# Last up product, first activations and first weights of down: one written order, and other tiles to load into

## The chip, the cores and the metric

The kernel runs on one core of a Trainium2 chip. What is compared is the time of one execution on the device, in microseconds (us). The core has TensorE (PE, with its weight loads shown apart as PEld), VectorE (DVE), ScalarE (ACT), GpSimd (POOL) and SyncE (SP), which issues most of the transfers. Each engine takes its own instructions in order and waits on semaphores for the others.

## The reference

One inference step of a one-layer decoder trunk: modulation from the conditioning vector, a norm, an input projection, a short convolution beside dilated window attention, an output projection with a gated residual, and then the part that this case is about:

```
h2 = rmsnorm(x, norm2_g) * (1 + sc2) + sh2          # x is [1056 tokens, 1024]
ffn = (silu(h2 @ w_gate) * (h2 @ w_up)) @ w_down    # w_gate, w_up [1024, 2816]; w_down [2816, 1024]
x = x + ga2 * ffn
y = rmsnorm(x, final_g)
```

1024 tokens are the prompt and 32 are the samples. Everything is float32.

## The kernel before

Each float32 matrix product is made of three matmuls on operands that are split in two: a high part (names ending in `h` or `hi`), which ACT makes by a copy into a rounded type, and a low part (`l` or `lo`), which DVE makes by subtracting the high part from the original. A weight tile is loaded into a `raw` tile, ACT writes `wh` from it and DVE writes `wl`; an activation tile `a` gives `ah` and `al` in the same way. So a tile is ready for PE only after a transfer, one ACT and one DVE instruction.

**Gate and up.** The hidden width is walked in eleven steps `f` (0 to 10, `FH` = 11). For each `f`, `ffn_pair` makes the gate product and then the up product of two lanes (the two halves of the tokens), each with `block_product`. One `block_product` has seven steps; in each step a half `wh`, `wl` of a weight tile multiplies a block of each lane in 12 matmuls of 264 columns, and the sums go to PSUM banks 0, 1, 0, 2, 0, 2, 0 of the lane (named `pss`, `pspt`, `psmm`). The weights come through `weight_units`: the raw tiles `r1` (pool `wp`, three places) and `r2` (pool `w3`, three places) are loaded by SP, POOL makes sums and differences of their quarters, and ACT and DVE split them. After a step `hold` copies a bank by ACT (`p1`, `u2`, `p5` in the code, `p` and `u` in the profile), or `put` adds by DVE and multiplies into the tile `sg`. At the end of `f` POOL stores `sg` in DRAM (`a_d`).

**Down.** The eleven `f` form chunks of 3, 3, 3 and 2. For a chunk, `load_a` brings its activations back from `a_d` (for the first chunk six tiles of 128x1056) through places of the `raw` tag of `wp` and splits them into `ah` and `al`, which take the places of the operands of up (`ua`, `ub`). Then, for each of the eight column blocks `m`, `load_down` brings 128x768 weights through the same `raw` places, and `down` makes three blocks of tokens (384, 384 and 288) of 18 matmuls each; `add_gated` adds each block to a tile of the residual (`x2` in the code, `x` in the profile), which SP loads from `xT_d` in the first chunk. The PSUM tiles of down take turns between the tags of `psmm` (two places) and `pss` (three places).

**Order.** A scheduler orders the instructions of each engine at build time by its own estimates; `tc.high_priority()` moves work ahead, `in_order(x)` makes an instruction stand behind another, and `program_order()` makes the instructions of PE, DVE, ACT and POOL that are recorded inside it stand in the order in which the code records them (SP is not among them). The code of `load_a` and `load_down` stood after the whole of gate and up.

Of the kernel before, what the change touches and what calls it, by code (L numbers as in the profile page):

```python
# [59 lines left out]
def hybrid_step(  # L60
# [1257 lines left out]
    def weight_units(w, f):  # L1318

        with tc.high_priority():  # L1320
            r1 = load_raw(w[:, :, P * f:P * f + P], KT)
            r2 = w3.tile([P, KT, P], F32, tag="raw", bufs=3, name=nm("raw"))
            last_w[0] = nc.sync.dma_start(r2, w[:, :, P * (f + FH):P * (f + FH) + P])
            s1 = sw.tile([P, 4, P], F32, tag="sw", bufs=2, name=nm("sw"))
# [31 lines left out]

    def block_product(w, f, lanes, sgs, up, hook=None):

        units = weight_units(w, f)
        banks = [[ps("s") for _ in lanes], [ps("pt") for _ in lanes], [ps("mm") for _ in lanes]]  # L1360
# [28 lines left out]
        for step, bank in enumerate((0, 1, 0, 2, 0, 2, 0)):  # L1389
            wh, wl, k0 = next(units)  # L1390
            for i, s in enumerate(lanes):
# [24 lines left out]
            if hook and step == 2:  # L1416
                hook(last)
        with tc.high_priority():
# [9 lines left out]

    def ffn_pair(f, lanes, pool, bufs, hook=None):
# [16 lines left out]
    xb.release()  # L1446
    w2 = tc.alloc_tile_pool(name="w2", bufs=1, side="right", reuse_waits="tile")
    for f in range(1, FH):
        ffn_pair(f, [0, 1], w2, 4)
        if f == 4:  # L1450
# [27 lines left out]

    a_pools = [ua] * 12 + [ua] * 4 + [ub] * 8 + [ub] * 2 + [ua] * 10 + [ua] * 2 + [ub] * 6

    def load_a(c):

        out = []
        for f in range(CHUNKS[c][1]):
            for i in range(2):
                raw = wp.tile([P, T], F32, tag="raw", bufs=3, name=nm("a"))
                nc.sync.dma_start(raw, a_d[c][:, i, f])
                ah = unit(a_pools.pop(0), "ah", dt=F32R)
                al = unit(a_pools.pop(0), "al", dt=F32R)
                with tc.high_priority():  # L1490
                    act(ah, raw)
                    nc.vector.tensor_sub(al, raw, ah.bitcast(F32))
                out.append((i, f, ah, al))
        return out

    def load_down(f0, nf, m):

        with tc.high_priority():
            raw = wp.tile([P, T], F32, tag="raw", bufs=3, name=nm("raw"))
            r = raw[:, :D].rearrange("p (k c) -> p k c", c=P)  # L1500
            for i in range(2):
                nc.sync.dma_start(r[:, nf * i:nf * i + nf], w_d_v[:, i, f0:f0 + nf, P * m:P * m + P])
            return split_raw(r, 2 * nf)

    def down(w, a, nf, m, t0, n):
# [7 lines left out]

    a = load_a(0)
    fg = d2.tile([P, D], F32, name="fg")
    nc.gpsimd.dma_start(fg, bcast(final_g, 0, P))
    for c, (f0, nf) in enumerate(CHUNKS):
        if f0 + nf < FH:
            for m in range(KT):
                w = load_down(f0, nf, m)  # L1520
                if c == 0:
# [3 lines left out]
                for t0, n in TBS:  # L1525
                    down(w, a, nf, m, t0, n)
            a = load_a(c + 1)
            continue
# [65 lines left out]
```

## Time and profile before

| | |
|---|---|
| median of 3 runs | 1378.84 us (1377.95 to 1380.05) |
| the profiled execution | 1376.94 us |
| its span, first to last instruction | 1375.2 us |
| mean granted TensorE clock | 0.966 of full speed |
| busy share of PE, DVE, ACT, POOL | 95%, 52%, 36%, 15% |

The profile is one execution. Times of single instructions are counted from the start of its span; the 1.74 us that the execution takes beyond the span lie around it.

### The profile page before, as it was taken

The numbers are of one execution on the slowest core, as the hardware profiler recorded it, in microseconds if no ns is written. First come the engines' busy times: TensorE is split into PE (matmuls) and PEld (weight loads), VectorE is DVE, ScalarE is ACT, GpSimd is POOL, SyncE is SP. The second block draws the span as 40 slices with busy tenths as digits, with TensorE's granted clock in tenths as the row PEclk, the third lists the DMA queues.
The fourth block names the chain that finished last, engine by engine and source line by source line (L and its number), as shares of the span: only waits on it lengthen the run. The fifth ranks groups of instructions, "written<-read, shape, count | busy, mean of one in ns | idle before, by whom it ended". The sixth has DMA issues, their size and how long they took to land.

```text
span 1375.2 us, 23628 instructions
## 1 busy us (share of the span) xinstructions
PE 1307.9 (95%) x9488; PEld 1206.0 (88%) x9488; DVE 716.9 (52%) x1448; ACT 499.6 (36%) x1077; POOL 212.1 (15%) x235
## 2 busy tenths in 40 slices
PE   8999998999899999996999999999999599999996
PEld 7767686859588979995999999999999599999996
DVE  5732364137324968779554465554454435353465
ACT  5442515242423325636333344333344302020244
POOL 3700000000000001232323233332231000000000
PEclk9999999969899999998999999999999899999998
DMA  9957474337463965783436344332451534141343
GB/s 315 310 194 256 147 256 151 93 101 255 123 182 103 236 217 168 245 261 109 143 120 231 100 184 132 108 109 83 162 188 61 197 132 141 47 141 47 95 152 128
DMA packets 188093, 220.80 MB, mean 161 GB/s; under 512 B 12426, under 2 KB 159367, under 8 KB 187472
## 3 DMA queue, kind: packets, MB, share of 16 engines
q1 hardware_dynamic: 169550, 173.89, 39.5%
q0 software_dynamic: 11504, 41.96, 9.1%
q10 hardware_dynamic: 6930, 3.45, 1.0%
q8 instruction: 74, 1.21, 0.4%
q14 instruction: 35, 0.29, 0.1%
HBM read 182.11 MB, written 64.21 MB: 179 GB/s over the span
## 4 chain that ended last, share of the span: by engine, by line
PE 73%; DVE 9%; issue 8%; DMA 7%; POOL 2%; ACT 1%; SPq 1%; DVEq 0%; POOLq 0%; ACTq 0%
PE pss L1398 6%; PE pss L1397 6%; PE pss L1396 6%; PE psmm L162 4%; PE psmm L163 4%; PE psmm L164 4%; PE pss L1509 3%; PE pss L1510 3%; PE pss L1511 3%; PE psmm L1509 3%; PE psmm L1510 3%; PE psmm L1511 3%; PE psmm L1397 3%; PE psmm L1396 3%; PE psmm L1398 3%
## 5 line engine op out<-in xcount | busy, mean ns | idle before, releaser
L93 ACT ACTIVATE wh<-raw 128x512 fp32r<-128x512 f32 (+2 forms) x200 | 152.7, 775 | 440.4 <-PE psmm L163 91.2
L1396 PE MATMUL pss<-xh,wh 128*128 128x264 f32 x704 | 201.1, 286 | 12.8 <-ACT wh L93 9.6
L1398 PE MATMUL pss<-xh,wl 128*128 128x264 f32 x704 | 201.2, 286 | 3.7 <-DVE wl L1333 3.4
L1397 PE MATMUL pss<-xl,wh 128*128 128x264 f32 x704 | 200.8, 285 | 0.0
L162 PE MATMUL psmm<-hh,wh 128*128 128x384 f32 (+1 forms) x528 | 176.9, 335 | 0.0
L163 PE MATMUL psmm<-hl,wh 128*128 128x384 f32 (+1 forms) x528 | 175.8, 333 | 0.0
L164 PE MATMUL psmm<-hh,wl 128*128 128x384 f32 (+1 forms) x528 | 174.7, 331 | 0.0
L137 DVE TENSOR_TENSOR wl<-raw,wh 128x1024 fp32r<-128x1024 f32 (+2 forms) x103 | 107.3, 1043 | 97.8 <-ACT wh L93 54.1
L1333 DVE TENSOR_TENSOR wl<-raw,wh 128x512 fp32r<-128x512 f32 x96 | 89.2, 940 | 118.3 <-ACT wh L93 117.0
L1396 PEld LDWEIGHTS pss<-xh,wh 128*128 128x128 f32 x704 | 133.4, 190 | 13.7 <-ACT wh L93 9.8
L1398 PEld LDWEIGHTS pss<-xh,wl 128*128 128x128 f32 x704 | 132.9, 189 | 5.0 <-DVE wl L1333 4.4
L1397 PEld LDWEIGHTS pss<-xl,wh 128*128 128x128 f32 x704 | 133.4, 189 | 0.0
L162 PEld LDWEIGHTS psmm<-hh,wh 128*128 128x128 f32 x528 | 100.8, 191 | 14.7 <-issue 11.5
L163 PEld LDWEIGHTS psmm<-hl,wh 128*128 128x128 f32 x528 | 100.9, 191 | 5.3 <-issue 4.9
L164 PEld LDWEIGHTS psmm<-hh,wl 128*128 128x128 f32 x528 | 101.4, 192 | 3.1 <-issue 2.8
L1396 PE MATMUL psmm<-xh,wh 128*128 128x264 f32 x352 | 101.0, 287 | 0.3 <-ACT wh L93 0.2
L1397 PE MATMUL psmm<-xl,wh 128*128 128x264 f32 x352 | 100.6, 286 | 0.0
L1398 PE MATMUL psmm<-xh,wl 128*128 128x264 f32 x352 | 100.1, 285 | 0.0
L1509 PE MATMUL pss<-ah,wh 128*128 128x384 f32 (+1 forms) x264 | 86.2, 326 | 14.7 <-ACT wh L93 14.7
L1510 PE MATMUL pss<-al,wh 128*128 128x384 f32 (+1 forms) x264 | 85.8, 325 | 0.0
L1511 PE MATMUL pss<-ah,wl 128*128 128x384 f32 (+1 forms) x264 | 85.7, 325 | 0.0
L1509 PE MATMUL psmm<-ah,wh 128*128 128x384 f32 (+1 forms) x264 | 85.4, 324 | 0.0
(324 smaller groups left out, 2896.8 us busy)
## 6 DMA issues: line engine op xcount, KB each, us to landing
ring<-in_w_ada_dram SPq DMA_DIRECT2D x32, 512.0 KB
out_dram<-in_cache_kv_dram SPq DMA_DIRECT2D x8, 2040.0 KB
raw<-in_w_in_dram SPq DMA_DIRECT2D x24, 512.0 KB
raw<-in_w_gate_dram SPq DMA_DIRECT2D x24, 512.0 KB
raw<-in_w_up_dram SPq DMA_DIRECT2D x24, 512.0 KB
a_d<-sg POOLq DMA_DIRECT2D x22, 528.0 KB, 3.3
a<-a_d SPq DMA_DIRECT2D x22, 528.0 KB
raw<-in_w_down_dram SPq DMA_DIRECT2D x48, 192.0 KB
```

Source lines behind the costliest of these rows:

```text
L93: return nc.scalar.activation(out, in_, func, **kw)
L137: nc.vector.tensor_sub(wl[:, :nk], raw[:, :nk], wh[:, :nk].bitcast(F32))
L162: nc.tensor.matmul(out, wh[:, k], h, start=(i == 0), stop=False)
L163: nc.tensor.matmul(out, wh[:, k], l, start=False, stop=False)
L164: last = nc.tensor.matmul(out, wl[:, k], h, start=False, stop=(i == n - 1))
L1333: nc.vector.tensor_sub(wl[:, 4 * i:4 * i + 4], x, h.bitcast(F32))
L1396: nc.tensor.matmul(o, wh[:, k0 + k], hi[:, k], start=st, stop=False, skip_group_check=True)
L1397: nc.tensor.matmul(o, wh[:, k0 + k], lo[:, k], start=False, stop=False, skip_group_check=True)
L1398: last = nc.tensor.matmul(o, wl[:, k0 + k], hi[:, k], start=False, stop=(k == 3), skip_group_check=True)
L1509: nc.tensor.matmul(o[:, :n], wh, ah[:, t0:t0 + n], start=(j == 0), stop=False)
L1510: nc.tensor.matmul(o[:, :n], wh, al[:, t0:t0 + n], start=False, stop=False)
L1511: nc.tensor.matmul(o[:, :n], wl, ah[:, t0:t0 + n], start=False, stop=(j == 2 * nf - 1))
```

## The change

The last up product (`f` = 10) is recorded inside `program_order()`, and the loads and splits of the first chunk of down are called from its steps through the new argument `after`: the loads of four activation tiles begin at step 0, their splits follow steps 2, 3 and 4, the weights of the first column block (`begin_weights`) and the last two activation tiles follow steps 5 and 6. Two of the first four tiles are loaded into places of `w3`, which were those of the second weight tile; for that the tiles of `w3` become as wide as those of `wp` (1056 columns instead of 1024). The weight splits of that up product are fetched ahead in the code as well.

```
-            r2 = w3.tile([P, KT, P], F32, tag="raw", bufs=3, name=nm("raw"))
+            r2 = w3.tile([P, T], F32, tag="raw", bufs=3, name=nm("raw"))[:, :D].rearrange("p (k c) -> p k c", c=P)
...
-            wh, wl, k0 = next(units)
+            fetch(step + 1)
+            wh, wl, k0 = got[step]
...
+            if after:
+                if step % 2:
+                    fetch(min(step + 4, 7))
+                for run in after.get(step, ()):
+                    run()
...
-        block_product(w_u_v, f, lanes, sgs, True)
+        with program_order() if after else nullcontext():
+            block_product(w_u_v, f, lanes, sgs, True, after=after)
...
+    def raw_a(c, n, pool=None):
+        raw = (pool or wp).tile([P, T], F32, tag="raw", bufs=3, name=nm("a"))
+        return raw, nc.sync.dma_start(raw, a_d[c][:, n % 2, n // 2])
...
+    def begin_loads():
+        for n in range(4):
+            raw, last_a[0] = raw_a(0, n, (wp, wp, w3, w3)[n])
+            raws.append(raw)
+    def begin(n):
+        return lambda: begun.append(load_a(0, n, raws.pop(0) if raws else None))
+    def begin_weights():
+        first_w.append(load_down(*CHUNKS[0], 0))
+        last_a[0] = None
+    entry = {0: [begin_loads], 2: [begin(0), begin(1)], 3: [begin(2)], 4: [begin(3)], 5: [begin_weights, begin(4)],
+             6: [begin(5)]}
     for f in range(1, FH):
-        ffn_pair(f, [0, 1], w2, 4)
+        ffn_pair(f, [0, 1], w2, 4, after=entry if f == FH - 1 else None)
...
-    a = load_a(0)
+    a = begun
...
-                w = load_down(f0, nf, m)
+                w = load_down(f0, nf, m) if c + m else first_w[0]
```

ACT, from the second `u2` copy of the last up product to the first weights of down, before (1654 to 1665 are tiles of that up product, the `ah` are the activations of down, `wh_1685` its first weights):

```order
L93 ACTIVATE u2_1659_11460<-pss_1644_11354 128x264
L93 ACTIVATE p5_1660_11474<-psmm_1647_11357 128x264
L93 ACTIVATE wh_1664_11552<-raw_1650_11361 128x512
L93 ACTIVATE p5_1661_11488<-psmm_1648_11358 128x264
L93 ACTIVATE ah_1667_11596<-a_1666_11594 128x1056
L93 ACTIVATE ah_1670_11602<-a_1669_11600 128x1056
L93 ACTIVATE ah_1673_11608<-a_1672_11606 128x1056
L93 ACTIVATE ah_1676_11614<-a_1675_11612 128x1056
L93 ACTIVATE ah_1679_11620<-a_1678_11618 128x1056
L93 ACTIVATE ah_1682_11626<-a_1681_11624 128x1056
L93 ACTIVATE wh_1685_11635<-raw_1684_11632 128x768
```

And now (`wh_1679` are the first weights of down):

```order
L93 ACTIVATE u2_1665_11474<-pss_1651_11373 128x264
L93 ACTIVATE ah_1666_11476<-a_1658_11406 128x1056
L93 ACTIVATE ah_1668_11480<-a_1659_11408 128x1056
L93 ACTIVATE p5_1670_11496<-psmm_1654_11376 128x264
L93 ACTIVATE p5_1671_11510<-psmm_1655_11377 128x264
L93 ACTIVATE wh_1672_11512<-raw_1644_11355 128x512
L93 ACTIVATE ah_1674_11516<-a_1660_11410 128x1056
L93 ACTIVATE ah_1676_11548<-a_1661_11412 128x1056
L93 ACTIVATE wh_1679_11583<-raw_1678_11580 128x768
L93 ACTIVATE ah_1682_11589<-a_1681_11587 128x1056
L93 ACTIVATE ah_1685_11621<-a_1684_11619 128x1056
```

Two `ah` moved ahead of the `p5` copies and of the last weight split of up, and the first weights of down moved from behind six `ah` to behind four.

DVE, the end of the last up product before (the two `sg` rows are its last):

```order
L1370 TENSOR_TENSOR sg_1618_11122<-sg_1618_11122,pss_1643_11353 128x264
L1370 TENSOR_TENSOR sg_1619_11123<-sg_1619_11123,pss_1644_11354 128x264
L1492 TENSOR_TENSOR al_1668_11597<-a_1666_11594,ah_1667_11596 128x1056
L1492 TENSOR_TENSOR al_1671_11603<-a_1669_11600,ah_1670_11602 128x1056
L1492 TENSOR_TENSOR al_1674_11609<-a_1672_11606,ah_1673_11608 128x1056
L1492 TENSOR_TENSOR al_1677_11615<-a_1675_11612,ah_1676_11614 128x1056
L1492 TENSOR_TENSOR al_1680_11621<-a_1678_11618,ah_1679_11620 128x1056
L1492 TENSOR_TENSOR al_1683_11627<-a_1681_11624,ah_1682_11626 128x1056
L137 TENSOR_TENSOR wl_1686_11636<-raw_1684_11632,wh_1685_11635 128x768
```

And the last rows of that stretch now; above them stand, in this order, `al_1667`, `al_1669`, the last weight split of up (`wl_1673`), `al_1675` and four rows for `p5`:

```order
L1478 TENSOR_TENSOR al_1677_11549<-a_1661_11412,ah_1676_11548 128x1056
L1376 TENSOR_TENSOR u2_1664_11460<-psmm_1654_11376,u2_1664_11460 128x264
L1377 TENSOR_TENSOR sg_1618_11122<-sg_1618_11122,u2_1664_11460 128x264
L1376 TENSOR_TENSOR u2_1665_11474<-psmm_1655_11377,u2_1665_11474 128x264
L1377 TENSOR_TENSOR sg_1619_11123<-sg_1619_11123,u2_1665_11474 128x264
L137 TENSOR_TENSOR wl_1680_11584<-raw_1678_11580,wh_1679_11583 128x768
L1478 TENSOR_TENSOR al_1683_11590<-a_1681_11587,ah_1682_11589 128x1056
L1377 TENSOR_TENSOR sg_1618_11122<-sg_1618_11122,pss_1650_11372 128x264
L1377 TENSOR_TENSOR sg_1619_11123<-sg_1619_11123,pss_1651_11373 128x264
L1478 TENSOR_TENSOR al_1686_11622<-a_1684_11619,ah_1685_11621 128x1056
L137 TENSOR_TENSOR wl_1694_11708<-raw_1692_11704,wh_1693_11707 128x768
```

All six `al` stood behind the last row of up; now five of them and the first weights of down stand among its rows, and one behind.

SP, the loads of the first chunk of down before (`a` activations, `raw` weights, `x2` residual; `x2` means two transfers only at a row's end):

```order
L1487 DMA a_1672_11606<-a_d0_83 128x1056
L1523 DMA x2_1687_11639<-xT_d_82 128x1056
L1487 DMA a_1675_11612<-a_d0_83 128x1056
L1487 DMA a_1678_11618<-a_d0_83 128x1056
L1487 DMA a_1681_11624<-a_d0_83 128x1056
L1523 DMA x2_1695_11711<-xT_d_82 128x1056
L1502 DMA raw_1684_11632<-in_w_down_dram 128x3x128 x2
L1502 DMA raw_1692_11704<-in_w_down_dram 128x3x128 x2
L1523 DMA x2_1703_11783<-xT_d_82 128x1056
```

And now:

```order
L1468 DMA a_1661_11412<-a_d0_83 128x1056
L1488 DMA raw_1678_11580<-in_w_down_dram 128x3x128 x2
L1468 DMA a_1681_11587<-a_d0_83 128x1056
L1468 DMA a_1684_11619<-a_d0_83 128x1056
L1488 DMA raw_1692_11704<-in_w_down_dram 128x3x128 x2
L1488 DMA raw_1700_11776<-in_w_down_dram 128x3x128 x2
L1488 DMA raw_1708_11848<-in_w_down_dram 128x3x128 x2
L1488 DMA raw_1716_11920<-in_w_down_dram 128x3x128 x2
L1557 DMA x2_1687_11639<-xT_d_82 128x1056
L1557 DMA x2_1695_11711<-xT_d_82 128x1056
```

The first weights moved ahead of the last two activations, and the first residual tile moved from the fourth place of these loads to behind five weight tiles.

## Rows read from the trace of the kernel before

**Rows 1.** The page, busy time, share of the span and instructions of each engine.

```profile
PE 1307.9 (95%) x9488; PEld 1206.0 (88%) x9488; DVE 716.9 (52%) x1448; ACT 499.6 (36%) x1077; POOL 212.1 (15%) x235
```

**Rows 2.** Windows: us, busy by engine (instructions), then PEclk, DMA share, GB/s.

```profile
720.00:1080.00 360.00, 359.26 (x2951) 358.26 (x2950) 181.63 (x289) 140.14 (x288) 102.89 (x87) 1.00 0.39 133
1101.00:1360.00 259.00, 259.00 (x1630) 258.12 (x1629) 123.92 (x237) 61.76 (x102) 0.00 (x0) 1.00 0.37 112
```

**Rows 3.** Waits of PE from 1097 us on: total us, times, longest.

```profile
PE pspt L1467 <- DVE yo L1475: 2.7, 1, 2.7
```

**Rows 4.** Timeline of PE, 1082.2 to 1101.2 us: start, length, instruction, [idle <-releaser].

```profile
1082.40 0.28 PE L1398 MATMUL pss<-xh,wl 128*128 128x264 f32 x1
1097.35 0.69 PE L1509 MATMUL pss<-ah,wh 128*128 128x384 f32 x1 [14.67 <-ACT wh L93]
...
1100.68 0.34 PE L1509 MATMUL pss<-ah,wh 128*128 128x384 f32 x1
```

**Rows 5.** Windows around the gap, columns as in rows 2.

```profile
1085.00:1086.00 1.00, 0.00 (x0) 0.00 (x0) 1.00 (x2) 0.00 (x0) 0.26 (x1) 1.00 1.06 300
...
1087.00:1090.00 3.00, 0.00 (x0) 0.00 (x0) 0.00 (x0) 0.78 (x1) 0.00 (x0) 0.50 1.00 393
```

**Rows 6.** The chain that ended last, 1083 to 1098 us: start, us, what.

```profile
1084.34 4.86 DMA a<-a_d
...
1092.06 4.01 DMA raw<-in_w_down_dram
```

**Rows 7.** Timeline of ACT, 1071 to 1079 us.

```profile
1071.08 0.39 ACT L93 ACTIVATE u<-pss 128x264 f32<-128x264 f32 x1 [1.07 <-PE pss L1398]
...
1073.87 0.63 ACT L93 ACTIVATE wh<-raw 128x512 fp32r<-128x512 f32 x1 [0.96 <-PE psmm L1397]
1074.41 0.37 ACT L93 ACTIVATE p<-psmm 128x264 f32<-128x264 f32 x1
1074.68 3.02 ACT L93 ACTIVATE ah<-a 128x1056 fp32r<-128x1056 f32 x3
```

**Rows 8.** Timeline of DVE, 1074 to 1084.5 us.

```profile
1074.54 0.69 DVE L1333 TENSOR_TENSOR wl<-raw,wh 128x512 fp32r<-128x512 f32 x1 [4.20 <-ACT wh L93]
...
1079.81 0.43 DVE L1369 TENSOR_TENSOR u<-psmm,u 128x264 f32<-128x264 f32 x1 [0.55 <-PE psmm L1398]
1080.28 0.43 DVE L1370 TENSOR_TENSOR sg<-sg,u 128x264 f32<-128x264 f32 x1
...
1083.06 2.42 DVE L1492 TENSOR_TENSOR al<-a,ah 128x1056 fp32r<-128x1056 f32 x2
```

**Rows 9.** Timeline of DVE, 1018 to 1115 us.

```profile
1063.72 1.22 DVE L1333 TENSOR_TENSOR wl<-raw,wh 128x512 fp32r<-128x512 f32 x1 [2.07 <-ACT wh L93]
...
1098.92 0.96 DVE L137 TENSOR_TENSOR wl<-raw,wh 128x768 fp32r<-128x768 f32 x1 [0.63 <-ACT wh L93]
1102.45 0.62 DVE L1141 SCALAR_TENSOR_TENSOR x<-pss,modt,x 128x384 f32<-128x384 f32 x1 [2.57 <-PE pss L1511]
```

**Rows 10.** Timeline of PE, 1079 to 1083 us: the first matmul of the last step.

```profile
1079.61 0.28 PE L1396 MATMUL pss<-xh,wh 128*128 128x264 f32 x1
```

**Rows 11.** Timeline of SP's queue, 1029 to 1096 us.

```profile
1029.69 41.00 SPq L1487 DMA_DIRECT2D a<-a_d  x3
1075.26 0.32 SPq L1523 DMA_DIRECT2D x<-xT_d  x1
1084.34 2.66 SPq L1487 DMA_DIRECT2D a<-a_d  x3
```

**Rows 12.** Transfers of 528 KB by tile a_d, issue to landing; the third late activation on ACT.

```profile
DMA to landing us min/median/max: 3.1/3.3/5.0
1093.67 1.08 ACT L93 ACTIVATE ah<-a 128x1056 fp32r<-128x1056 f32 x1 [2.09 <-DMA a<-a_d]
```

**Rows 13.** Timeline of ACT, 1159 to 1180 us: one weight split of down for each block.

```profile
1176.92 0.85 ACT L93 ACTIVATE wh<-raw 128x768 fp32r<-128x768 f32 x1 [7.83 <-PE pss L1510]
```

**Rows 14.** Timeline of POOL, 1061 to 1066 us.

```profile
1063.10 1.29 POOL L1343 TENSOR_TENSOR raw<-raw 128x512 f32<-128x512 f32 x1
```

More of the change, by code (lines that the diff above doesn't have):

```diff
@@ L1355, in weight_units, with block_product, fetch @@
         yield u[0]
-    def block_product(w, f, lanes, sgs, up, hook=None):
-        units = weight_units(w, f)
+    def block_product(w, f, lanes, sgs, up, hook=None, after=None):
+        units, got = weight_units(w, f), []
+        def fetch(n):
+            while len(got) < n:
+                got.append(next(units))
+        if after:
+            fetch(3)
         banks = [[ps("s") for _ in lanes], [ps("pt") for _ in lanes], [ps("mm") for _ in lanes]]
@@ L1417, in block_product @@
                 hook(last)
+            if after:
+                if step % 2:
+                    fetch(min(step + 4, 7))
+                for run in after.get(step, ()):
+                    run()
         with tc.high_priority():
@@ L1427, in block_product, with ffn_pair @@
                     nc.sync.dma_start(dst, src)
-    def ffn_pair(f, lanes, pool, bufs, hook=None):
+    def ffn_pair(f, lanes, pool, bufs, hook=None, after=None):
         sgs = [pool.tile([P, 2, NSUB], F32, tag="sg", bufs=bufs, name=nm("sg")) for _ in lanes]
         block_product(w_g_v, f, lanes, sgs, False, hook)
-        block_product(w_u_v, f, lanes, sgs, True)
+        with program_order() if after else nullcontext():
+            block_product(w_u_v, f, lanes, sgs, True, after=after)
         for s, sg in zip(lanes, sgs):
@@ L1447, in hybrid_step, with load_a, load_down @@
     w2 = tc.alloc_tile_pool(name="w2", bufs=1, side="right", reuse_waits="tile")
+    a_pools = [ua] * 12 + [ua] * 4 + [ub] * 8 + [ub] * 2 + [ua] * 10 + [ua] * 2 + [ub] * 6
+    last_a = [None]
+    def raw_a(c, n, pool=None):
+        raw = (pool or wp).tile([P, T], F32, tag="raw", bufs=3, name=nm("a"))
+        return raw, nc.sync.dma_start(raw, a_d[c][:, n % 2, n // 2])
+    def load_a(c, n, raw=None):
+        if raw is None:
+            raw, _ = raw_a(c, n)
+        ah = unit(a_pools.pop(0), "ah", dt=F32R)
+        al = unit(a_pools.pop(0), "al", dt=F32R)
+        with tc.high_priority():
+            act(ah, raw)
+            nc.vector.tensor_sub(al, raw, ah.bitcast(F32))
+        return n % 2, n // 2, ah, al
+    def load_down(f0, nf, m):
+        with tc.high_priority():
+            raw = wp.tile([P, T], F32, tag="raw", bufs=3, name=nm("raw"))
+            r = raw[:, :D].rearrange("p (k c) -> p k c", c=P)
+            for i in range(2):
+                with in_order(last_a[0]):
+                    nc.sync.dma_start(r[:, nf * i:nf * i + nf], w_d_v[:, i, f0:f0 + nf, P * m:P * m + P])
+            return split_raw(r, 2 * nf)
+    begun, raws, first_w = [], [], []
+    def begin_loads():
[9 more added lines that the diff above has]
+             6: [begin(5)]}
     for f in range(1, FH):
-        ffn_pair(f, [0, 1], w2, 4)
+        ffn_pair(f, [0, 1], w2, 4, after=entry if f == FH - 1 else None)
         if f == 4:
@@ L1477, in final_rows @@
         nc.sync.dma_start(y_prompt[0, P * t:P * t + P] if t < 8 else y_sample.rearrange("b t f -> (b t) f"), yo[:n])
[L1479 to L1503, printed above, removed]
     def down(w, a, nf, m, t0, n):
@@ L1526, in hybrid_step @@
                     down(w, a, nf, m, t0, n)
-            a = load_a(c + 1)
+            a = [load_a(c + 1, n) for n in range(2 * CHUNKS[c + 1][1])]
             continue
```

## Prediction

> **What bounds the kernel now.** I read the page first: PE is busy 95% of the span [rows 1], so a change elsewhere pays only where it takes away time in which PE stands still or runs slowly. The windows tell where that is not: in the long stretch of gate and up before 1080 us PE is busy 359.26 of 360 us, and in down from 1101 to 1360 us 259 of 259 us, both at full granted clock [rows 2]. From 1097 us to the end the list of waits names, besides the wait at the start of down, one of 2.7 us in the final rows [rows 3]. So everything here hangs on one place. PE's timeline shows it: the last matmul of up starts at 1082.40, the first of down at 1097.35, after 14.67 us of waiting for ACT's `wh` [rows 4]. The clock granted to PE is still 1.00 three microseconds into the gap and 0.50, the lower level of 1.2 GHz, from 1087 us; after 1101 us it is 1.00 again [rows 2].
>
> The chain says what filled the gap: a load of `a` (4.86 us to land), its split, a transfer of down's weights (4.01 us) [rows 6], their split [rows 4]. They are late for a reason in the order: SP had brought three `a` by some microseconds after 1070 [rows 11], ACT had split them from 1074.68 [rows 7], but DVE took the first `al` only at 1083.06 [rows 8], behind its last row of up. Only then did a `raw` place come free, and three more `a` and the weights had to go through it, at 300 to 393 GB/s with the transfers' engines full [rows 5].
>
> **The change, part by part.** *The gap.* Up's matmuls follow each other by 359.26/2951 = 0.12 us [rows 2], so down could start at 1082.52. Gap: 1097.35 - 1082.52 = 14.83 us. *The clock.* A column block of down takes 0.85 + 7.83 = 8.68 us in steady state [rows 13], 36 matmuls of 384 columns and 18 of 288, so 8.68/49.5 = 0.175 us for a wide one. The first ten of down took 1100.68 - 1097.35 = 3.33 us [rows 4] instead of 1.75: 1.58 us lost. If PE never stands, both go: 16.4 us.
>
> *What PE waits for now.* I lay ACT's and DVE's new order on up's old step times. ACT copies the second `u2` until 1071.47; an `ah` takes 3.02/3 = 1.0 [rows 7], so two end at 1073.5; the `p5` copies (0.37), the second free once its bank is done, 48 matmuls before step 6, 1079.61 - 48 x 0.12 = 1073.8 [rows 10], end at 1074.4; up's last `wh` (0.63) at 1075.0; two more `ah` at 1077.0. The first `wh` of down takes a place that step 5 reads, and step 5's last bank is done at 1079.81 [rows 8]: 1079.8 to 1080.65 at 0.85 [rows 13]; the last two `ah` end at 1082.7. DVE: an `al` takes 2.42/2 = 1.21, a `wl` of up 0.69, a put row 0.47 from start to start [rows 8], a `wl` of down 0.96 [rows 9]. Two `al` 1072.6 to 1075.0; `wl` to 1075.7; `al` from 1076.0 to 1077.2; four put rows to 1079.1; `al` to 1080.3; four put rows to 1082.2; down's first `wl` to 1083.15; fifth `al` to 1084.35; two put rows to 1085.3; sixth `al` to 1086.5.
>
> Against PE: step 6 starts at 1079.61 [rows 10]; its `wl` is there at 1075.7, and the bank that it writes again is read by 1077.65. That `al` rows now stand ahead of up's own rows costs nothing, with 2 us to spare on DVE; if that cover is gone, each microsecond more is one of PE's. In down the fifth matmul reads the first `wl`: 1082.52 + 4 x 0.175 = 1083.22 against 1083.15. The 24th reads the sixth `al`: 1086.55 against 1086.5. Both are level, so I allow 0.3 us of waiting. Below nothing is excluded, since PE has no other gap here to give.
>
> *The transfers.* The third and fourth `a` now go into `w3` places that the products before left, so at the latest when this up began, 144 matmuls before step 6, 1062.3. Places of `wp` come free with the first two `al` (1073.9, 1075.1); a load of this size lands after 3.3 us [rows 12], so the last two `a` are there at 1078.4, and their `ah` stand at 1080.65 and later. Even with the 7.0 us of the third late `a` (issued at 1084.34 + 2.66 - 0.32 = 1086.68 [rows 11], used at 1093.67 [rows 12]) the last lands at 1082.1, about in time.
>
> *The residual tile.* It was issued at 1075.26 [rows 11]; now it stands on SP behind five weight tiles, the fifth of which waits for the second block's `wl`. Weights 2 are issued when down's first `wl` is done (two issues of some 0.4, as the 0.32 of [rows 11], 1083.2 to 1084.0), land in 4.0 as in the full stretch [rows 6] at most, 1088.0; split by 1089.9; PE wants them at 1082.52 + 8.68 = 1091.2. Weights 5 are issued to 1090.7, the tile at 1091.0, landing at 1094.3. Who needs it: its first two adds, 0.62 each [rows 9], free the `psmm` place that the third part of block 2 takes at 1091.2 + 36 x 0.175 = 1097.5. It is hidden by 2 us; with 7.0 instead of 3.3 us the wait is 1098.0 + 1.24 - 1097.5 = 1.7.
>
> One rule bears on this: the Trainium skill, DMA: Bandwidth & Descriptors, section Issuing engines are not separate DMA queues, says that transfers from SP and GpSimd run on the same 16 engines and interleave, so the two stores of `sg` and the load of `final_g` on POOL's queue slow SP's tiles just here. The trace agrees as far as it goes: the window of 1085 us holds such a store beside SP's loads, and the engines' share is 1.06 [rows 5]. By that rule the longer landing holds, and the sum would be 1.7 us worse.
>
> *The wider `w3` tile* adds no work and no column; *the same matmuls* stand on PE, only a few of the first block in another order; the two last `sg` stores move by 2 us to 1085.3, and only the last chunk reads them. Nothing.
>
> **Sum.** 1376.94 - 14.83 - 1.58 + 0.3 = 1360.8 us for an execution like the profiled one. That one lay 1.9 us under the median of the three runs, so I forecast 1362.7 us. About 0.2%, 2.8 us, is what a measurement of this kernel can tell from no change.
>
> **Rivals.** (a) *Something of the handover stays late.* DVE is full from 1072.6 to 1086.5, and a split of 0.69 us took 1.22 at 1063.72 [rows 9], beside work of POOL [rows 14]. If the fifth and sixth `al` ran so, they would take 1.9 us more; with both transfers of the residual's path at 7.0 us, weights 2 land at 1091.0, weights 5 go out by 1093.6, the tile lands at 1100.9 and the wait is 4.6 us. So 1.5 to 5 us stay: 1364 to 1367.5. For it: both margins are level; against it: POOL has nothing left to compute then, only two stores and a load to issue. Chance 0.15. (b) *The gap shrinks by half*: the first weights or one `a` miss and PE stands about 7 us, long enough for the clock to fall as it did: half of 16.4 stays, 1362.7 + 8.2 - 0.3 = 1370.6. For it speaks that one missing input holds all of down; against it that each is ready 2 us or more ahead but two. Chance 0.04. (c) *No change*: the order's waits sit in up instead, as much as the gap gives back, 1377 to 1380. It would need DVE 16 us late, and it is busy only 52% of the span [rows 1]. Chance 0.03. (d) *Slower*: the residual tile holds PE in block 2. It decides from a landing at 1097.5 - 1.24 + 16.4 = 1112.7 on, 22 us after its issue, where the longest landing read here is 7.0; at 25 us it is 1381. Chance 0.02. The rest, 0.76, is the forecast.
>
> **Numbers.** The forecast's own range is 1360.2 to 1364.3: no wait or 1 us, and the runs' spread of -0.9 and +1.2 about the median. Taking in the nearer part of (a) up to 1366 covers 8 in 10. Faster by over 0.2%: 0.76 + 0.15 + 0.04 = 0.95; within: 0.03; slower: 0.02.
>
> **What would show it.** Right: no PE wait over 0.5 us between the last up matmul and block 2, clock 1.00 throughout 1080 to 1100, `al` rows between up's put rows, first matmul of down 0.12 us after up's last. Wrong, and by how much: a wait of PE on `wl` or `al` near the fifth or 24th matmul of down (DVE is late), on the `x` add in block 2 (the residual tile), or in up's step 6 on DVE (the order costs up itself). A second gap later in down would mean that the time was only passed on.

## The result and the profile after

The changed kernel takes 1360.05 us (median of 4 runs, 1358.03 to 1362.42). The kernel before takes 1378.39 us (median of 4 runs, 1371.61 to 1380.05). The ratio is 0.9879, with a 95% interval from 0.985 to 0.9908, clear of 1: it is faster. The forecast of 1362.7 us was 2.65 us too high, its sign and its main mechanism right, and the median lies 0.15 us under the low end of the range.

The page of the profiled execution (1358.57 us, span 1356.8) answers to [rows 1]:

```profile
PE 1306.3 (96%) x9488; PEld 1205.2 (89%) x9488; DVE 716.3 (53%) x1448; ACT 498.7 (37%) x1077; POOL 211.6 (16%) x235
```

The work is the same and the span is shorter, so most of the time came out of PE's idle. PE's list of waits from 1075 us to the end answers to [rows 3] (engine, line and releaser: us in total, times, longest):

```profile
PE pspt L1527 <- DVE yo L1535: 2.7, 1, 2.7
```

The 14.67 us wait at the start of down is gone from it, and nothing new of that kind has come. PE's timeline at the same place as [rows 4] (start, length, instruction, in brackets the idle time before it):

```profile
1080.95 0.28 PE L1406 MATMUL pss<-xh,wl 128*128 128x264 f32 x1
1081.07 0.34 PE L1543 MATMUL pss<-ah,wh 128*128 128x384 f32 x1
...
1081.77 0.34 PE L1545 MATMUL pss<-ah,wl 128*128 128x384 f32 x1
...
1085.07 0.34 PE L1544 MATMUL pss<-al,wh 128*128 128x384 f32 x1
...
1095.88 0.34 PE L1545 MATMUL pss<-ah,wl 128*128 128x384 f32 x1
1096.32 0.40 PE L1543 MATMUL psmm<-ah,wh 128*128 128x288 f32 x1
```

Down's first matmul starts 0.12 us after up's last; the fifth stands at 1081.77 and the 24th at 1085.07, each on its unbroken spacing of 0.17. One crack is left: 1095.88 to 1096.32 is 0.44 us, 0.26 more than that spacing, at the third part of the second down product. The windows (us, busy by engine, then granted clock, DMA share, GB/s) answer to [rows 2] and [rows 5]:

```profile
720.00:1080.00 360.00, 359.26 (x2950) 358.26 (x2949) 185.87 (x291) 141.91 (x290) 102.59 (x87) 1.00 0.40 137
1080.00:1085.00 5.00, 5.00 (x34) 5.00 (x33) 4.00 (x6) 1.76 (x3) 1.40 (x2) 1.00 0.52 152
1085.00:1090.00 5.00, 5.00 (x35) 5.00 (x34) 0.96 (x1) 0.31 (x2) 0.56 (x1) 1.00 1.05 327
1090.00:1097.00 7.00, 6.89 (x41) 6.57 (x40) 2.83 (x6) 0.65 (x1) 0.00 (x0) 1.00 1.06 385
1101.00:1340.00 239.00, 239.00 (x1501) 238.13 (x1500) 116.02 (x216) 59.28 (x98) 0.00 (x0) 1.00 0.37 110
```

The clock stays at 1.00, its upper level of 2.4 GHz, and PE's 359.26 us up to 1080 are those of before: up pays nothing for the splits in it. DVE's timeline, against [rows 8], shows where these now stand:

```profile
1071.01 2.43 DVE L1478 TENSOR_TENSOR al<-a,ah 128x1056 fp32r<-128x1056 f32 x2 [2.14 <-ACT ah L93]
...
1076.43 0.43 DVE L1376 TENSOR_TENSOR p<-pss,p 128x264 f32<-128x264 f32 x1
1076.89 0.43 DVE L1377 TENSOR_TENSOR sg<-sg,p 128x264 f32<-128x264 f32 x1
1077.24 1.25 DVE L1478 TENSOR_TENSOR al<-a,ah 128x1056 fp32r<-128x1056 f32 x1
...
1080.03 0.95 DVE L137 TENSOR_TENSOR wl<-raw,wh 128x768 fp32r<-128x768 f32 x1
1080.90 1.25 DVE L1478 TENSOR_TENSOR al<-a,ah 128x1056 fp32r<-128x1056 f32 x1
1082.07 0.76 DVE L1377 TENSOR_TENSOR sg<-sg,pss 128x264 f32<-128x264 f32 x2
1082.75 1.25 DVE L1478 TENSOR_TENSOR al<-a,ah 128x1056 fp32r<-128x1056 f32 x1
...
1095.12 0.62 DVE L1141 SCALAR_TENSOR_TENSOR x<-pss,modt,x 128x384 f32<-128x384 f32 x1 [3.49 <-DMA x<-xT_d]
1095.66 0.61 DVE L1141 SCALAR_TENSOR_TENSOR x<-psmm,modt,x 128x384 f32<-128x384 f32 x1
```

Down's first `wl` is done at 1080.98, 0.79 us before the fifth matmul wants it; the sixth `al` at 1084.00, 1.07 us before the 24th. The first sum waits for the residual tile until 1095.12, and that is the crack: the second sum frees PE's place at 1096.27. SP's queue (against [rows 11]) shows the way of that tile:

```profile
1068.90 0.92 SPq L1488 DMA_DIRECT2D raw<-in_w_down_dram  x2
1072.29 1.51 SPq L1468 DMA_DIRECT2D a<-a_d  x2
1081.01 6.82 SPq L1488 DMA_DIRECT2D raw<-in_w_down_dram  x8
1087.92 2.13 SPq L1557 DMA_DIRECT2D x<-xT_d  x2
```

It is issued at 1087.92, behind eight halves of weights, and takes 1095.12 - 1087.92 = 7.20 us until its sum runs.

**A measure that holds still.** The time at which up ends differs from run to run by far more than the terms in dispute (last section). So I compare executions by *down's length*: from the start of up's last matmul to the start of the last transposes of the output, the only ones over 32 columns. These are, before and after:

```profile
1364.16 1.22 PE L1467 MATMUL pspt<-ident,x 128*32 128x128 f32 x5 [2.74 <-DVE yo L1475]
```

```profile
1346.73 0.49 PE L1527 MATMUL pspt<-ident,x 128*32 128x128 f32 x3 [2.74 <-DVE yo L1535]
```

Before: 1364.16 - 1082.40 [rows 4] = 281.76 us. After: 1346.73 - 1080.95 = 265.78 us. The difference of the spans, 1375.2 - 1356.8 = 18.40 us, is thus 1.45 ahead of down (1082.40 - 1080.95), 15.98 in down, and 0.97 behind the start of the last transposes; the first and the last of these lie in work that both kernels share. The first expectations count to the end of the span instead, so that they take in those last 10 to 11 us.

### The profile page after: what moved, and what is told of

The parts are those of the page before. It is cut to its first block, busy times and chain, and to the rows that moved or that the text cites. A ratio compares the mean times of both kernels' runs of the same rounds, so it can differ in the third digit from the quotient of the medians.

```text
span 1356.8 us, 23628 instructions
## 1 busy us (share of the span) xinstructions
PE 1306.3 (96%) x9488; PEld 1205.2 (89%) x9488; DVE 716.3 (53%) x1448; ACT 498.7 (37%) x1077; POOL 211.6 (16%) x235
## 4 chain that ended last, share of the span: by engine, by line
PE 72%; DVE 9%; issue 8%; DMA 7%; POOL 2%; ACT 1%; SPq 1%; DVEq 0%; POOLq 0%; ACTq 0%
PE pss L1406 6%; PE pss L1405 6%; PE pss L1404 6%; PE psmm L162 4%; PE psmm L163 4%; PE psmm L164 4%; PE psmm L1543 3%; PE psmm L1544 3%; PE psmm L1545 3%; PE pss L1544 3%; PE psmm L1405 3%; PE pss L1543 3%; PE pss L1545 3%; PE psmm L1404 3%; PE psmm L1406 3%
## 5 line engine op out<-in xcount | busy, mean ns | idle before, releaser
L1544 PE MATMUL psmm<-al,wh 128*128 128x384 f32 (+1 forms) x264 | 85.4, 323 | 0.0
```

The lines of the kernel that those rows point to most:

```text
L1544: nc.tensor.matmul(o[:, :n], wh, al[:, t0:t0 + n], start=False, stop=False)
```

## The experiments

The theory was: the gap stood because DVE took all `al` behind up's last row; early loads and the written order of the splits are both needed, the first weights must go ahead of the last two activations, and the two places beside the wide weights matter least. Rivals: the transfers alone made the gap; or the order alone did.

Down's length of one profiled execution of each kernel, and the ratio of its runs against runs of before beside them:

| kernel | down's length (us) | ratio (95%) |
|---|---|---|
| before | 281.76 | |
| after | 265.78 | 0.9879 (0.985 to 0.9908) |
| after, again | 267.10 | 0.9897 (0.9847 to 0.9948) |
| all splits late | 273.14 | 0.9973 (0.9936 to 1.0009) |
| without the written order | 273.51 | 0.9932 (0.99 to 0.9965) |
| two early tiles, not four | 267.95 | 0.9895 (0.9859 to 0.993) |
| before with early loads | 279.89 | 1.0014 (0.998 to 1.0048) |
| first weights last | 269.03 | 0.9917 (0.9883 to 0.9952) |
| 4.8 us more of DVE | 272.66 | one run, 1365.33 us |
| before, 60 idle-filling matmuls | 282.82 | 1.0013 (0.9991 to 1.0035) |
| before, 67 of them | 281.05 | 0.9988 (0.9946 to 1.0029) |
| residual tile first | 268.10 | 0.9898 (0.9852 to 0.9944) |
| the same, weights in order | 267.34 | 0.9866 (0.9787 to 0.9944) |
| the same, DVE in order too | 265.34 | 0.9865 (0.9807 to 0.9924) |

**All splits late.** The loads stay early; the splits are recorded behind up's last step.

```diff
-    entry = {0: [begin_loads], 2: [begin(0), begin(1)], 3: [begin(2)], 4: [begin(3)], 5: [begin_weights, begin(4)],
-             6: [begin(5)]}
+    entry = {0: [begin_loads], 6: [begin(0), begin(1), begin(2), begin(3), begin_weights, begin(4), begin(5)]}
```

> The changed kernel, but with all the splits of down's first six activation tiles and first weights recorded after up's last step, so that VectorE computes up's last puts first and then four al, the weights' low part, two al; the early loads into the four places stay as they are. Read by the time from up's last matmul to the end of the span (292.80 us in the profiled run before, 275.85 after) and by TensorE's wait there. Theory (VectorE's order held the gap, and early loads alone don't remove it): VectorE starts on the al some 0.5 us before up's last matmul ends and needs four al of 1.25 and the weights' 0.95, so the weights' low part is there about 5.5 us after up's last matmul, where the fifth down matmul wants it after 0.8: 4 to 6 us more than after, about 1365 us, with a TensorE wait of 3.5 to 6 us. Rival (only the late loads made the gap): 0 to 0.5 us more than after, 1360 us, and no TensorE wait over 0.5 us.

DVE and then PE of this kernel, whose last up matmul starts at 1066.40:

```profile
1066.72 0.43 DVE L1377 TENSOR_TENSOR sg<-sg,pss 128x264 f32<-128x264 f32 x1 [1.04 <-PE pss L1406]
1067.06 4.76 DVE L1478 TENSOR_TENSOR al<-a,ah 128x1056 fp32r<-128x1056 f32 x4
1071.74 0.95 DVE L137 TENSOR_TENSOR wl<-raw,wh 128x768 fp32r<-128x768 f32 x1
```

```profile
1068.37 0.45 PE L1543 MATMUL pss<-al,wh 128*128 128x384 f32 x1 [1.52 <-DVE al L1478]
1072.74 0.69 PE L1544 MATMUL pss<-ah,wl 128*128 128x384 f32 x1 [3.75 <-DVE wl L137]
```

Four `al` and the `wl` stand behind up's last row, and PE waits 1.52 + 3.75 = 5.27 us for them, within the 3.5 to 6 expected. (Such a wait is counted from the end of the matmul before; matmuls of 0.34 us start every 0.17, so each wait costs some 0.17 us more than is listed.) Down's length grows by 273.14 - 265.78 = 7.36 us, more than the 4 to 6 expected, for the slow clock comes on top: 0.50 from 1073 to 1076 us in this run. The rival that early loads are enough is out; so is the one that the order alone made the gap, for 8.62 of the 15.98 us stay saved with every split late. The order without early loads was not run.

**Without the written order.**

```diff
-        with program_order() if after else nullcontext():
-            block_product(w_u_v, f, lanes, sgs, True, after=after)
+        block_product(w_u_v, f, lanes, sgs, True, after=after)
```

> The changed kernel with its early loads, places and calls at the same steps, but without the written order over the last up block: the scheduler orders each engine, and puts VectorE's al behind up's last puts again. Theory: the same as with all splits recorded late, 4 to 6 us more than after (about 1365 us), with a TensorE wait of 3.5 to 6 us at the start of down, since recording the calls between up's steps moves nothing unless the order holds. Rival (early loads are enough): 0 to 0.5 us more than after.

Up's last matmul starts at 1079.24. PE waits 1.52 and 3.75 us for the same two rows, the second at

```profile
1085.59 0.69 PE L1544 MATMUL pss<-ah,wl 128*128 128x384 f32 x1 [3.75 <-DVE wl L137]
```

and down's length is 273.51. Recording the calls between up's steps moves nothing on DVE by itself; the scheduler puts them back behind the last row, and the written order is the part that moves them.

**Two early tiles, not four.**

```diff
-        for n in range(4):
-            raw, last_a[0] = raw_a(0, n, (wp, wp, w3, w3)[n])
+        for n in range(2):
+            raw, last_a[0] = raw_a(0, n, wp)
```

> The changed kernel, but only the first two activation tiles are loaded early, into the places that it uses for them anyway; the third and fourth are loaded when their split is reached, into the same pool, so the two places beside the wide weights are not used. The order of splits is as in the changed kernel. Theory (the order of the splits is what counts, and two early places keep it fed): 0 to 1.5 us more than after, 1360 to 1361.5 us, and 276 to 277.5 us from up's last matmul to the end. Rival (the two more places carry it): the third tile's place comes free only after the splits of the first, its load of about 3 to 5 us lands after the puts, and VectorE's later al stand behind it: 4 to 8 us more, 1364 to 1368 us, with a TensorE wait of several us in the first down product.

Down's length is 267.95, 2.17 over the first run of the changed kernel and 0.85 over its repeat: nearer to the theory than to the rival, but 277.99 us to the end of the span, 0.49 over the theory's range. Up's last matmul starts at 1083.51 here; ACT's timeline and then PE's show two places:

```profile
1085.71 1.09 ACT L93 ACTIVATE ah<-a 128x1056 fp32r<-128x1056 f32 x1 [1.79 <-DMA a<-a_d]
```

```profile
1100.73 0.40 PE L1543 MATMUL psmm<-ah,wh 128*128 128x288 f32 x1 [1.35 <-DVE x L1141]
```

The sixth `ah` starts 2.20 us after up's last matmul where the changed kernel has both late ones done by 1081.02, 0.07 after; its `al` ends at 1088.10, 4.59 after. The 18th down matmul waits for that `ah` and the 24th for that `al`, which by then is 0.5 us late in all. So the two added places are worth about half a microsecond. The 1.35 is the residual tile, which varies by itself (below).

**Before with early loads.** The kernel before, and of the change only the four early loads with their places.

```diff
+    for n in range(4):
+        first_raws.append((wp, wp, w3, w3)[n].tile([P, T], F32, tag="raw", bufs=3, name=nm("a")))
+        nc.sync.dma_start(first_raws[n], a_d[0][:, n % 2, n // 2])
...
+    for n in range(4):
+        begun.append(split_a(n % 2, n // 2, first_raws[n]))
```

> The kernel before, with one thing of the change alone: the first four activation tiles of down are loaded early into the two places of their own pool and the two beside the wide weights. VectorE's order is that of before, the six al behind up's last puts and the weights' low part behind all of them, and the weights are loaded behind the last two tiles. Theory (places and order each hold a part of the gap): the loads of four tiles leave the gap but two more loads, the weights' load and VectorE's chain stay: a gap of 8 to 11 us where before shows 14.83, 1369 to 1375 us. Rival 1 (the transfers alone made the gap): under 2 us are left, 1360 to 1362 us. Rival 2 (the order alone made it): the gap stays 13 to 15 us, 1377 to 1379 us.

Up's last matmul starts at 1078.19. The chain that ended last and ACT's timeline show down's first weights, then PE's timeline the start of down:

```profile
1081.74 7.22 DMA raw<-in_w_down_dram
```

```profile
1089.34 0.84 ACT L93 ACTIVATE wh<-raw 128x768 fp32r<-128x768 f32 x1 [2.94 <-DMA raw<-in_w_down_dram]
```

```profile
1090.23 0.69 PE L1521 MATMUL pss<-ah,wh 128*128 128x384 f32 x1 [11.77 <-ACT wh L93]
```

The gap is 12.04 - 0.12 = 11.92 us, over the 8 to 11 expected and under the 13 to 15 of the order alone. Five `al` are done by 1084.78, but the weights come last: their place comes free at 1081.28 with the second `al`, behind up's last row, they then take 7.22 us to land, and that sets the start. Down's length falls by only 1.87 us. Beside the run with all splits late this prices a part that neither the prediction nor its rivals had by itself: there the weights go ahead, and 281.76 - 273.14 = 8.62 us are saved. The 6.75 us between the two are put down to the weights' turn; they also differ in the written order of up's other rows, which was not taken apart.

**First weights last.** The changed kernel with that turn undone.

```diff
-    entry = {0: [begin_loads], 2: [begin(0), begin(1)], 3: [begin(2)], 4: [begin(3)], 5: [begin_weights, begin(4)],
-             6: [begin(5)]}
+    entry = {0: [begin_loads], 2: [begin(0), begin(1)], 3: [begin(2)], 4: [begin(3)], 5: [begin(4)],
+             6: [begin(5), begin_weights]}
```

> The changed kernel, with the first weights of down loaded and split behind the last two activation tiles instead of ahead of them (loads and VectorE's and ScalarE's order both); all else as in the changed kernel. Theory (VectorE's place of the weights' low part counts, the fifth down matmul needs it): it is ready behind the last al, 3 to 4 us after up's last matmul instead of at it, and if the weights' transfer is later too, later by that: TensorE waits 2.5 to 4 us at the fifth or at the first matmul of down, 1362 to 1365 us. Rival (the order within the six is of no account as long as all are in up's rows): 0 to 0.5 us more than after.

DVE's timeline of this kernel, and then PE's:

```profile
1086.31 0.95 DVE L137 TENSOR_TENSOR wl<-raw,wh 128x768 fp32r<-128x768 f32 x1
```

```profile
1087.32 0.45 PE L1545 MATMUL pss<-ah,wl 128*128 128x384 f32 x1 [1.84 <-DVE wl L137]
```

Up's last matmul starts at 1084.21; the `wl` is done 1087.26 - 1084.21 = 3.05 us after up's last matmul. PE had two more matmuls to do without it and waits 1.84 us, less than the 2.5 expected; with the clock at 0.59 from 1088 to 1091 us, down is 3.25 us longer (its median, 1365.93 us, is over the 1362 to 1365 expected). In the changed kernel the weights' transfer is early in either order: with the first `al` ahead of up's last rows a place comes free in time, and the weights go out at 1076.72 here. So less hangs on their turn than in the kernel before.

**4.8 us more of DVE.**

```diff
             nc.vector.tensor_sub(al, raw, ah.bitcast(F32))
+            for _ in range(4 if (c, n) == (0, 3) else 0):
+                nc.vector.tensor_sub(al, raw, ah.bitcast(F32))
```

> The changed kernel, with VectorE's subtraction for the fourth activation tile repeated four times over (same result), about 4.8 us more of VectorE ahead of up's puts of the third column block. It measures how much room VectorE's chain has: in the changed kernel the low part of the first weights is done 0.79 us before the fifth down matmul wants it, and the last al 1.1 us before. Theory (the chain of VectorE sets the start of down as soon as it is later than its 0.79 us): TensorE waits some 4 us in all in the first down product, and with a clock that falls in such a wait 4 to 6 us more from up's last matmul to the end than after's 275.85. Rival (VectorE has more room than that, because its work waits for something else anyway): under 1 us.

Up's last matmul starts at 1080.82. The added rows on DVE, and then PE's two waits:

```profile
1078.39 5.13 DVE L1480 TENSOR_TENSOR al<-a,ah 128x1056 fp32r<-128x1056 f32 x4
```

```profile
1083.93 0.45 PE L1545 MATMUL psmm<-ah,wh 128*128 128x384 f32 x1 [2.48 <-DVE u L1376]
1086.07 0.69 PE L1547 MATMUL pss<-ah,wl 128*128 128x384 f32 x1 [1.52 <-DVE wl L137]
```

The waits add to 4.00 us, as 4.8 less the margin of 0.79 would have it, but this is in part luck: the added rows took 5.13 us, not 4.8, and the matmul at 1086.07 stands 5.25 us after up's last instead of 0.82, so 4.43 us late, near 5.13 - 0.79 = 4.34. The first wait comes at a place that I had not named: the third down matmul takes a bank that up's late row on DVE still has to read. Down's length is 6.88 us more than after's, over the 4 to 6 expected; the rest goes with a slow clock again, 0.50 from 1086 to 1090 us.

**The clock by itself.** The kernel before, its gap filled with matmuls that nobody reads.

```diff
+    def fill_gap(n):
+        o = ps("o")
+        prev = last_mm[0]
+        for j in range(n):
+            with tc.issue_after(prev.ins):
+                prev = nc.tensor.matmul(o[:, :P], ident, ones, start=True, stop=True, skip_group_check=True)
...
+    fill_gap(60)
```

> The kernel before, with 60 matmuls added that nobody reads (128x128, in a chain of program order behind up's last matmul, into a bank that is free there), so that TensorE works through a good part of the gap; nothing else moves. It takes the clock's term out of the gap's. Theory (the slow first ten matmuls of down come from the idle gap before them): the wait for the first weights ends at the same distance from up's last matmul as in before (15 us, of which TensorE now fills a part), and where the added matmuls last until down starts, down's first ten matmuls take 1.7 to 1.8 us instead of 3.33: 1.6 us less from up's last matmul to the end than before's 292.80. If the added matmuls end some us before down starts, a part of the 1.6 us or nothing is saved. Rival (the first matmuls are slow for another reason, as the weights' or the activations' arrival): 3.3 us again, at a granted clock of 1.00.

PE's timeline and then a window of this kernel:

```profile
1094.45 0.44 PE L1519 MATMUL pss<-ah,wh 128*128 128x384 f32 x1 [1.40 <-ACT wh L93]
```

```profile
1096.00:1099.00 3.00, 3.00 (x12) 3.00 (x11) 0.28 (x1) 0.00 (x0) 0.00 (x0) 0.51 0.78 229
```

The filling ended 1.40 us early, and the clock fell all the same, behind the start of down instead of ahead of it. Nothing was gained: 282.82 us. A second kernel with 67 covers that too:

> The kernel before with 67 unread matmuls instead of 60 behind up's last matmul. The 60 took 13.56 us, ended 1.40 us before the first weights were there, and after that wait of 1.40 us the granted clock fell all the same, 1.6 us into down, so that the slow matmuls stayed. With 67 the added work lasts about 15.1 us, up to the weights' coming (15.09 us behind up's last matmul). Theory (it is the wait just before down that lowers the clock, and TensorE busy throughout keeps it): wait under 0.3 us, granted clock 1.00 in the first 5 us of down, down's first ten matmuls in 1.7 to 2.0 us, and 280 to 280.6 us from up's last matmul to the last transposes where before has 281.76 and the run with 60 has 282.82. Rival (the added matmuls don't count as work for the clock, or down's first matmuls are slow for another reason): the clock falls to 0.50 behind down's start again, 281.7 to 283 us.

The window around the start of down:

```profile
1089.00:1094.00 5.00, 4.79 (x29) 4.39 (x29) 2.05 (x3) 1.56 (x2) 0.00 (x0) 1.00 0.88 282
```

Now the clock holds 1.00. Down's first ten matmuls take 1092.10 - 1089.77 = 2.33 us, with 0.21 of listed waiting for the `wl` in them, where before has 3.33 [rows 4]. Of the term of 1.58 us 1.00 is shown; the rest hangs on inputs that are ready, which they are not in this kernel. Down's length is 281.05, 0.71 less than before and less gain than the 1.2 to 1.8 us expected, since down also starts 0.20 us later.

**The repeat.** The changed kernel, unaltered.

> The changed kernel itself once more, beside the others on their chip, to see what repeats. Theory (the saving is one of down's start alone and does not vary): 265.5 to 266.1 us from up's last matmul to the last transposes, no wait but the 0.26 us one, and a ratio to before between 0.985 and 0.991, while the time of up's last matmul itself varies by several us from run to run. Rival (a part of the ratio came from the earlier stages of the runs compared): a ratio nearer 1 than 0.991 with the same 266 us.

PE's only wait in down's first products, in its timeline:

```profile
1093.43 0.41 PE L1543 MATMUL psmm<-ah,wh 128*128 128x288 f32 x1 [1.11 <-DVE x L1141]
```

Down's start repeats to the hundredth up to the second product; then the residual tile, issued 6.86 us after up's last matmul, takes 8.31 us until its sum (1092.23 - 1083.92), and PE's third part starts 1.27 us later than its spacing (1.11 of it listed as idle), where the first run had 0.26. Down's length is 267.10, so the theory that it does not vary is wrong: the two differ by 1.3 us. The ratio agrees.

**The residual tile first.** It is put ahead of the second weights in SP's order.

```diff
-                    nc.sync.dma_start(x, xT_d[:, m])
+                    first = nc.sync.dma_start(x, xT_d[:, m])
+                    last_a[0] = first if m == 0 else last_a[0]
```

> The changed kernel, with one transfer moved: the first residual tile is issued ahead of the second and later weights of down, where the changed kernel issues it behind four of them (at 1087.92 us). It tests the one wait that the changed kernel has left there, 0.26 us at the third part of the second down product for a sum that waits for this tile. Theory (the residual tile's landing is the last thing that down waits for at its start): that wait is gone, the first sum starts right behind the first down product, and 0.2 to 0.4 us less from up's last matmul to the end, too little for the median to show. Rival (weights that come later cost more than the residual tile gives): a wait for the second or third weights' low part of 0.5 us or more.

PE's timeline of this kernel, at the second down product:

```profile
1083.55 0.44 PE L1543 MATMUL psmm<-ah,wh 128*128 128x384 f32 x1 [1.69 <-ACT wh L93]
```

The rival was right: the wait for the tile went, a wait of 1.69 us for the second weights came, since the scheduler now mixed the halves of two weight tiles. Keeping the weights in order:

```diff
-                    nc.sync.dma_start(r[:, nf * i:nf * i + nf], w_d_v[:, i, f0:f0 + nf, P * m:P * m + P])
+                    load = nc.sync.dma_start(r[:, nf * i:nf * i + nf], w_d_v[:, i, f0:f0 + nf, P * m:P * m + P])
+                last_a[0] = load if f0 == 0 else None
```

> The changed kernel with the first residual tile issued ahead of the second weights of down, as in the run that moved it before, but with the weights of the first chunk kept in their order (the two halves of one column block next to each other), which that run mixed: there the second weights landed 9.7 us after TensorE's first down matmul and TensorE waited 1.7 us. Read by the time from up's last matmul to the last transposes of the output (281.76 us before, 265.78 after). Theory (the residual tile is the one late thing left, and the mixed halves made the wait of the earlier run): no TensorE wait of over 0.2 us in the first two down products, 265.3 to 265.7 us. Rival (the residual tile ahead of the weights delays them too much whatever their order): a wait of 0.5 us or more at the second down product, 266.3 us or more.

DVE's timeline of this kernel, behind the first down product:

```profile
1086.62 0.19 DVE L1147 TENSOR_TENSOR x<-x,gs 128x32 f32<-128x32 f32 x1
1086.73 1.83 DVE L137 TENSOR_TENSOR wl<-raw,wh 128x768 fp32r<-128x768 f32 x2
```

Again a wait of 1.25 us, and for a third reason: on DVE the second weights' `wl` now stood behind all sums of the first product, though its `wh` had started at 1080.84. So the last run also fixes DVE's order there:

```diff
+        with in_order(sum_after[0]):
             nc.vector.scalar_tensor_tensor(x[:, :n_p], o[:, :n_p], modt[:, w, m, 0:1], x[:, :n_p],
...
+                    if m == 0:
+                        next_w = load_down(f0, nf, 1)
+                        sum_after[0] = last_wl[0]
```

> The changed kernel with the first residual tile issued ahead of the second weights, the weights of the first chunk in their order, and with VectorE's order fixed there: low part of the second weights, the three sums of the first down product, low part of the third weights. In the run before, the scheduler put the second weights' low part behind the three sums once the tile came early, and TensorE waited 1.25 us for it; here it stands ahead of them. It is to show whether what the changed kernel has left in its second down product (0.26 us in its first profiled run, 1.11 in the repeat) can be had. Theory (the tile and the weights both have time enough, and only VectorE's order made the new waits): no TensorE wait of 0.3 us or more in down's first three products, 265.4 to 265.9 us from up's last matmul to the last transposes, against 265.78 and 267.10 of the changed kernel. Rival (what is brought forward on the full queues makes something else late by as much again): a wait of 0.5 us or more there, 266.3 to 267.5 us.

SP and DVE of it:

```profile
1069.00 0.32 SPq L1563 DMA_DIRECT2D x<-xT_d  x1
```

```profile
1079.14 0.96 DVE L138 TENSOR_TENSOR wl<-raw,wh 128x768 fp32r<-128x768 f32 x1 [1.87 <-ACT wh L93]
1080.01 0.61 DVE L1143 SCALAR_TENSOR_TENSOR x<-pss,modt,x 128x384 f32<-128x384 f32 x1
1080.81 0.62 DVE L1143 SCALAR_TENSOR_TENSOR x<-psmm,modt,x 128x384 f32<-128x384 f32 x1 [0.19 <-PE psmm L1548]
```

No wait is left in down's first products, and down's length is 265.34, the shortest of all: 0.44 and 1.76 us less than the two runs of the changed kernel. Its median, 1351.78 us beside 1375.1 for before, gives a ratio whose interval overlaps that of the changed kernel, so by times alone it is not shown to be faster than that.

## Why the prediction was right, point by point

**The gap and the clock.** Counted from up's last matmul, down's 25th starts after 20.72 us before and after 4.30 in the changed kernel: 16.42 us, against a sum of 14.83 + 1.58 = 16.4. These matmuls are, before and after:

```profile
1103.12 0.34 PE L1509 MATMUL psmm<-ah,wh 128*128 128x384 f32 x1
```

```profile
1085.25 0.33 PE L1545 MATMUL pss<-ah,wl 128*128 128x384 f32 x1
```

The sum of both terms holds; the clock's is also shown by itself, as to 1.00 of its 1.58 us.

**DVE.** "Both are level" was too cautious. From the first `al` to the last DVE took 1084.00 - 1071.01 = 12.99 us, where I had laid out 13.9: two put rows follow each other in 0.81 (1075.62 to 1076.43), not 0.94. The margins were 0.79 and 1.07 us, and the added work cost about what 0.79 leaves of it. Of the 0.3 us that I allowed, nothing was spent on DVE.

**The residual tile.** One step failed: "It is hidden by 2 us". The tile went out sooner than I had it (6.97 us after up's last matmul, not 8.6), but its sum ran 7.20 and 8.31 us later, not 3.3. The upper bound, 7.0, was the right term: with it, and the tile going out 1.6 us sooner, its wait of 1.7 us comes to about 0.1, at the place where 0.26 and 1.27 us were lost. The Trainium skill, DMA: Bandwidth & Descriptors, section Issuing engines are not separate DMA queues, says that transfers started by different engines run on the same 16 DMA engines and interleave. The windows agree, with a DMA share of 1.05 and 1.06 from 1085 to 1097 us, and the load of `final_g` on POOL's queue, issued beside the tile at 1088.12, took 7.2 us as well. That POOL's transfers lengthened the landing, as the prediction has it, is not shown: from 1080 to 1100 us SP's own queue takes 68.0% of the engines' time and POOL's 23.3%, and no run separates them. (The POOL instruction in the first window of [rows 5] is the issue of `final_g`'s load at 1085.74, not a store; that load had waited for the last store to land.)

**The sum.** Down's saving was 15.98 us in one run and 281.76 - 267.10 = 14.66 in the other, for 16.1 forecast, so the repeat reaches to the near end of rival (a). For a run like the profiled one I had 1360.8; it took 1358.57, and the 2.2 us between are the 1.45 us ahead of down and the 0.97 behind it, less what the residual tile kept. These two are scatter of work that the change does not touch. The range was too narrow: it took -0.9 and +1.2 us about the median of three runs as the kernel's scatter, while the fourth run of before took 1371.61 and later ones went down to 1359.94. Nor do its terms give it: no wait or 1 us, with that spread, is 1361.5 to 1364.6, not 1360.2 to 1364.3, so the median lies 1.45 us under the range as worked out. The base was the larger error. Later runs of before have medians from 1374.75 to 1375.8; 16.1 less than these is 1358.6 to 1359.7, beside 1360.05 and 1358.80 for the changed kernel.

**The rivals.** No second gap came in down (239.00 of 239.00 us busy from 1101), none in up. Half of the gap, as in (b), is what stays when the splits are late: 7.36 us. Of (d), the residual tile cost 1.27 us at most in the changed kernel, not the 16.4 that it needs. Its example is 1 us off: a landing of 25 us would make 1382, not 1381. By the prediction's own signs the first run is right throughout, and the repeat shows the wait that it named for the residual tile.

## What to carry over

When one stage's end stands between the next stage's inputs and their use, early loads are not enough: ask on each in-order engine what the split stands behind, and in the queue what the first weights stand behind. Here the vector engine's order was worth 7.4 us, the weights' turn about 6.8 us while the splits were late and 3.3 with them early, and the extra places half a microsecond. Moving one transfer forward under a scheduler changes the order of other rows as well: two of three tries gave back the wait somewhere else, until the rows next to it were fixed too.

## What the runs showed beyond that

Up's last matmul starts between 1066.40 and 1084.21 us in executions of programs that are the same up to the last up block, and most of that is made ahead of the gate and up products. The first matmul of these that waits for its weights (the wait itself is the same) stands at

```profile
634.41 0.59 PE L1396 MATMUL pss<-xh,wh 128*128 128x264 f32 x1 [9.55 <-ACT wh L93]
```

in the kernel before, and in the run with all splits late at

```profile
619.41 0.59 PE L1404 MATMUL pss<-xh,wh 128*128 128x264 f32 x1 [9.53 <-ACT wh L93]
```

The granted clock from 200 to 400 us is 0.89 in the first and 0.96 in the second. So two medians here don't tell 5 us apart, as the 0.9973 and 0.9932 of two kernels with the same two waits show, and a length within one trace does. What sets the clock there was not tried.

A wait of 1.40 us was followed by 3 us at half clock, one of 1.69 us (the residual tile first) by none: 1.00 from 1082 to 1088 us. What makes the difference stays open.
